# Seven block products in place of eight in the gate and up projections of a two-layer encoder trunk

## The chip, the core and the metric

The kernel runs on one core of a Trainium2 chip. The metric is the device time of one execution in microseconds. Before the change three runs took 2505.06 us in the median (2503.48 to 2505.37). About 0.2% (5 us) is what a measurement of this kernel can tell from no change.

## What is computed

Two groups of tokens, a prompt of 1024 and a sample of 32, go through a trunk of two layers of width 1024. The first layer mixes tokens with an mLSTM (a matrix-memory recurrence over chunks), the second with windowed attention. Each mixer is followed by a gated feed-forward block, and each of the four sub-layers ends in a layer norm. The part that the change touches is the feed-forward block:

```python
def swiglu(x, w_gu, w_down):
    g, u = jnp.split(x @ w_gu, 2, axis=-1)      # w_gu 1024 x 5632
    return (jax.nn.silu(g) * u) @ w_down        # w_down 2816 x 1024
...
x = layer_norm(DEEPNORM_ALPHA * x + swiglu(x, w_gu[layer], w_down[layer]), ln_g[layer, 1], ln_b[layer, 1])
```

Everything is float32.

## The kernel before, in words

**Layout.** Features lie on the partitions. The activations `act` are eight feature tiles of 128, each for three token groups of 384, 384 and 288 columns (`GRP`). A float32 product is made from exact halves: every operand is split into a high part in float32r and the remainder, and `gemm` (line 251) issues three matmuls for each 128-row step of the contraction: high by high (L256), low of the activations or weights by high (L257, L258). A product of a 128-wide weight tile with one group over 1024 features is therefore 24 matmuls.

**Weights.** The class `Weights` (line 110) streams units of 128 x 1024 in the order of their use through two raw buffers (`RAW`). A split is a copy on ScalarE (L143, tile `wh`) and a subtraction on GpSimd (L145, tile `wl`; a few on VectorE). A ring holds four split units. `done` frees a unit and splits the next while fewer than three live. Four of the eight units of an output projection get homes outside the ring.

**Feed-forward** (`ffn`, line 813). There are 22 tiles of 128 hidden features. For each tile and group, `up_group` makes the gate product and the up product (24 matmuls each), applies Silu on ScalarE (L827), multiplies on VectorE (L829) and splits the result into `hh` (L830, ScalarE) and `hl` (L831, VectorE). Tiles are taken in blocks of 2, 4, 4, 4, 4, 4. After the tiles of a block and the first tile of the next, `down` multiplies the block's hidden tiles with the down weights, for each of the eight output tiles and each group, and VectorE adds every result to `act` (L873 in the first block, L875 later). The products go through three PSUM banks (`psdense`). The last block's down products are in `norm_tail`, interleaved with the layer norm.

**Order of work.** The program is written out by hand, each engine takes its instructions in program order, and side work (norm, recurrence, attention) is a generator that `gemm` advances by a few instructions after each step of three matmuls (`Weave.tick`, which counts an estimate of the time). An instruction that waits holds up what is behind it on its engine.

Of the kernel before, what the change touches and what calls it, by code (L numbers as in the profile page):

```python
# [16 lines left out]
P = 128  # L17
# [14 lines left out]
BLOCKS = (2, 4, 4, 4, 4, 4)  # L32
# [6 lines left out]
RAW = 2  # L39
# [9 lines left out]
# token groups: moving columns of one matrix product  # L49
# [60 lines left out]
class Weights:  # L110
    """Streams weight units [128, w] and splits each into two float32r parts whose sum is exact."""

    def __init__(self, nc, pool, units):
        self.nc, self.pool, self.units = nc, pool, units
        self.nload = self.nsplit = 0
        self.raw, self.parts, self.home, self.live = {}, {}, {}, set()
        self.on_vector = set()

# [9 lines left out]

    def split_to(self, i):
        while self.nsplit <= i and self.nsplit < len(self.units):  # L130
            u = self.nsplit
            w = self.units[u].shape[-1]
            if u not in self.home and len(self.live) == 4:
                return
            self.load_to(u)
            r = self.raw.pop(u)
            if u in self.home:
                hi, lo = self.home[u]
            else:
                self.live.add(u)  # L140
                hi = self.pool.tile([P, WD], F32R, name=f"wh{u}", tag="wh", bufs=4)
                lo = self.pool.tile([P, WD], F32R, name=f"wl{u}", tag="wl", bufs=4)
            self.nc.scalar.copy(hi[:, :w], r[:, :w])  # L143
            eng = self.nc.vector if u in self.on_vector else self.nc.gpsimd
            eng.tensor_sub(lo[:, :w], r[:, :w], hi[:, :w].bitcast(F32))  # L145
            self.parts[u] = (hi, lo)
            self.nsplit += 1
            self.load_to(u + RAW)

    def get(self, u):  # L150
        self.split_to(u)
        return self.parts[u]

    def done(self, u):
        self.parts.pop(u)
        self.live.discard(u)
        while len(self.live) < 3 and self.nsplit < len(self.units) and self.nsplit - u < 12:
            self.split_to(self.nsplit)
# [3 lines left out]
def kernel(ctx: ExitStack, tc: tile.TileContext, A, O):  # L162
# [63 lines left out]
    W = Weights(nc, base, units)  # L226
    W.on_vector.update(U_Q[:1] + U_KV + U_QB[:1])

# [20 lines left out]
    scr_g, scr_x = per_tile(lambda g, n: dram.tile([P, KT, n], F32, name=f"scrx{g}"))  # L249

    def gemm(out, lhs, rhs):
        """out (+)= lhs.T @ rhs in float32 from exact halves: hi*hi + hi*lo + lo*hi."""
        last = len(lhs) - 1
        us = 3 * (max(out.shape[-1], 256) / 2400.0 + 0.003)
        for k, ((ah, al), (bh, bl)) in enumerate(zip(lhs, rhs)):
            nc.tensor.matmul(out, ah, bh, start=(k == 0), stop=False)  # L256
            nc.tensor.matmul(out, ah, bl, start=False, stop=False)  # L257
            nc.tensor.matmul(out, al, bh, start=False, stop=(k == last))  # L258
# [6 lines left out]
    def wcols(u, m=P):  # L265
        hi, lo = W.get(u)
        return [(hi[:, k * m : (k + 1) * m], lo[:, k * m : (k + 1) * m]) for k in range(KT)]
# [1005 lines left out]
```

## Time and profile before

| of the profiled execution | |
|---|---|
| span, first to last instruction (its own time) | 2505.9 us |
| median of the three timed runs | 2505.06 us |
| mean granted TensorE clock | 0.982 |
| TensorE busy | 2419.2 us, 14946 matmuls |
| VectorE / ScalarE / GpSimd busy | 939.1 / 786.6 / 696.2 us |
| HBM traffic over the span | 51 GB/s |

Matmuls overlap in the pipeline: a 128x384 matmul shows as some 340 ns but they start about 173 ns apart. The time that one costs is the distance between starts. Idle time of VectorE, ScalarE and GpSimd costs nothing by itself; what counts is whether TensorE waits.

### The profile page before, as it was taken

How to read it: one execution, taken by the hardware profiler on the slowest of the kernel's cores; microseconds unless marked ns; L12 is line 12 of the kernel's file. 1: busy time of each engine (PE TensorE's matmuls, PEld its weight loads, DVE VectorE, ACT ScalarE, POOL GpSimd, SP SyncE). 2: the span in 40 equal slices, each digit the busy share in tenths (PEclk: the TensorE clock that was granted, in tenths of full speed). 3: DMA queues.
4: the chain of work that ended last, by engine and by line, in shares of the span. 5: the costliest groups of instructions: out<-in, count | busy, mean ns of one | idle time of the engine just before them, and what ended most of it. 6: DMA issues, size and time to landing. Idle time of an engine off the chain costs nothing.

```text
span 2505.9 us, 36370 instructions
## 1 busy us (share of the span) xinstructions
PE 2419.2 (97%) x14946; PEld 2321.5 (93%) x14946; DVE 939.1 (37%) x2240; ACT 786.6 (31%) x1719; POOL 696.2 (28%) x545
## 2 busy tenths in 40 slices
PE   8999998999999999999979999898999999999997
PEld 8899898999999999999968888798999999999996
DVE  4444466542121212112275777655212121111227
ACT  3443444351211111121155677526121111212123
POOL 2443322341221312121253333225222121311222
PEclk9999999999999999999988999899999999999999
DMA  3221213011111111111121000210111110211111
GB/s 133 65 65 51 51 39 126 26 34 51 51 51 34 60 37 57 34 51 34 60 83 52 28 27 28 84 45 26 60 39 63 34 60 26 68 34 34 51 43 70
DMA packets 58901, 129.36 MB, mean 52 GB/s; under 512 B 8624, under 2 KB 32488, under 8 KB 58352
## 3 DMA queue, kind: packets, MB, share of 16 engines
q1 hardware_dynamic: 57008, 122.72, 15.0%
q10 hardware_dynamic: 1728, 4.33, 0.4%
q8 instruction: 117, 1.92, 0.3%
q14 instruction: 48, 0.39, 0.1%
HBM read 117.61 MB, written 9.41 MB: 51 GB/s over the span
## 4 chain that ended last, share of the span: by engine, by line
PE 85%; DVE 6%; ACT 3%; issue 2%; DMA 2%; POOL 2%; SPq 0%; POOLq 0%; DVEq 0%; ACTq 0%
PE d L256 26%; PE d L258 26%; PE d L257 25%; PE psS L1020 2%; PE T L1066 1%; PE psS L1019 1%; DMA wib<-scrw 1%; DVE sxl L280 1%; POOL wl L145 1%; DVE act L334 1%; PE O L1081 1%; PE O L1082 1%; DMA act<-in_x 1%; ACT junk L681 1%; PE ln L319 0%
## 5 line engine op out<-in xcount | busy, mean ns | idle before, releaser
L256 PE MATMUL d<-sxh,wh 128*128 128x384 f32 (+1 forms) x2928 | 971.2, 332 | 11.2 <-ACT sxh L279 7.1
L257 PE MATMUL d<-sxl,wh 128*128 128x384 f32 (+1 forms) x2928 | 950.0, 324 | 6.0 <-DVE sxl L280 6.0
L258 PE MATMUL d<-sxh,wl 128*128 128x384 f32 (+1 forms) x2928 | 952.4, 325 | 2.1 <-POOL wl L145 2.1
L145 POOL TENSOR_TENSOR wl<-wr,wh 128x1024 fp32r<-128x1024 f32 x170 | 408.7, 2417 | 1308.3 <-ACT wh L143 1286.5
L256 PEld LDWEIGHTS d<-sxh,wh 128*128 128x128 f32 x2928 | 555.9, 190 | 26.0 <-ACT sxh L279 7.7
L258 PEld LDWEIGHTS d<-sxh,wl 128*128 128x128 f32 x2928 | 556.1, 190 | 12.3 <-POOL wl L145 12.3
L257 PEld LDWEIGHTS d<-sxl,wh 128*128 128x128 f32 x2928 | 556.4, 190 | 9.0 <-DVE sxl L280 8.0
L829 DVE TENSOR_TENSOR t<-t,d 128x384 f32<-128x384 f32 x132 | 68.7, 521 | 781.9 <-PE d L258 780.0
L256 PE MATMUL d<-hh,wh 128*128 128x384 f32 (+1 forms) x1056 | 345.6, 327 | 10.6 <-DVE act L368 10.6
L257 PE MATMUL d<-hl,wh 128*128 128x384 f32 (+1 forms) x1056 | 342.6, 324 | 0.0
L258 PE MATMUL d<-hh,wl 128*128 128x384 f32 (+1 forms) x1056 | 342.2, 324 | 0.0
L143 ACT CAST wh<-wr 128x1024 fp32r<-128x1024 f32 (+1 forms) x174 | 177.3, 1046 | 257.6 <-PE d L257 195.6
L830 ACT CAST hh<-t 128x384 fp32r<-128x384 f32 x132 | 64.2, 486 | 506.3 <-DVE t L829 506.3
L256 PEld LDWEIGHTS d<-hh,wh 128*128 128x128 f32 x1056 | 199.3, 189 | 12.6 <-DVE act L368 11.5
L257 PEld LDWEIGHTS d<-hl,wh 128*128 128x128 f32 x1056 | 199.6, 189 | 1.1 <-issue 0.3
L258 PEld LDWEIGHTS d<-hh,wl 128*128 128x128 f32 x1056 | 199.4, 189 | 0.5 <-POOL wl L145 0.5
L875 DVE TENSOR_TENSOR act<-act,d 128x384 f32<-128x384 f32 (+1 forms) x192 | 100.1, 521 | 262.7 <-PE d L258 262.7
L827 ACT ACTIVATE t<-d 128x384 f32<-128x384 f32 x132 | 61.3, 465 | 398.6 <-PE d L258 398.5
L1042 POOL TENSOR_SCALAR s<-s,st 128x256 f32<-128x256 f32 (+2 forms) x72 | 65.6, 911 | 157.5 <-DVE st L1041 107.8
L831 DVE TENSOR_TENSOR hl<-t,hh 128x384 fp32r<-128x384 f32 x132 | 72.4, 548 | 77.2 <-ACT hh L830 77.2
L256 PE MATMUL d<-wh,sxh 128*128 128x256 f32 (+3 forms) x288 | 87.3, 303 | 0.0
L258 PE MATMUL d<-wh,sxl 128*128 128x256 f32 (+3 forms) x288 | 81.6, 283 | 0.0
(183 smaller groups left out, 2639.2 us busy)
## 6 DMA issues: line engine op xcount, KB each, us to landing
wr<-in_gu SPq DMA_DIRECT2D x88, 512.0 KB, 3.2
wr<-in_dn SPq DMA_DIRECT2D x44, 512.0 KB, 3.3
act<-in_x SPq DMA_DIRECT2D x3, 1536.0 KB, 8.0
wr<-in_wqk SPq DMA_DIRECT2D x8, 512.0 KB, 3.5
nm<-scrm SPq DMA_DIRECT2D x32, 128.0 KB, 4.0
wr<-in_wo SPq DMA_DIRECT2D x8, 512.0 KB, 4.3
wr<-in_wout_a SPq DMA_DIRECT2D x8, 512.0 KB, 3.2
wr<-in_wqb SPq DMA_DIRECT2D x8, 512.0 KB, 3.3
```

Source lines behind the costliest of these rows:

```text
L143: self.nc.scalar.copy(hi[:, :w], r[:, :w])
L145: eng.tensor_sub(lo[:, :w], r[:, :w], hi[:, :w].bitcast(F32))
L256: nc.tensor.matmul(out, ah, bh, start=(k == 0), stop=False)
L257: nc.tensor.matmul(out, ah, bl, start=False, stop=False)
L258: nc.tensor.matmul(out, al, bh, start=False, stop=(k == last))
L827: nc.scalar.activation(t, pg, AF.Silu)
L829: nc.vector.tensor_mul(t, t, pu)
L830: nc.scalar.copy(hh[i][:, t0 : t0 + n], t)
L831: nc.vector.tensor_sub(hl[i][:, t0 : t0 + n], t, hh[i][:, t0 : t0 + n].bitcast(F32))
L875: nc.vector.tensor_add(z[:], z[:], ps)
L1020: nc.tensor.matmul(psS[h][:R, lo:256], q[r, h, tk], KL[g2][r, kc], start=False, stop=True)
L1042: nc.gpsimd.tensor_scalar_mul(p[:R, 0, lo:256], p[:R, 0, lo:256], st[:R, 2, 0:1])
```

## The change

For 18 of the 22 tiles (2 to 19) the gate and up weights of a tile are one matrix of 2 x 2 blocks: gate tile over the first and the second 512 features (a1, a2), up tile likewise (b1, b2). The two groups of 384 tokens are the other matrix: X11, X21 (group 0, first and second 512 features), X12, X22 (group 1). Instead of eight block products the tile takes seven, each with one of seven weight factors: a1·X11, a2·X21, s2·T2, b2·T4, s1·T1, s3·T3 and s4·X22, where s1 = b1 + b2, s2 = s1 - a1, s3 = a1 - b1, s4 = a2 - s2, T1 = X12 - X11, T2 = X22 - T1, T3 = X22 - X12, T4 = X21 - T2. Group 2 (288 tokens) has its four block products as before, with a1, a2, b1, b2. Sums of products are made partly by accumulating in one PSUM bank (`A`), partly by copies on ScalarE and additions on VectorE.

- The T's are made once in each layer, at the start of the feed-forward block, by two generators (`comb`, `comb_4`). T1 is written over X12, whose split halves are first stored to DRAM and loaded back before tiles 20 and 21.
- The s's are made for every tile on VectorE, in place in the raw weight buffers (four operations of 128 x 512).
- A weight unit is now split in two halves of 128 x 512, each with its own ring slot. The ring has six half slots where there were four whole ones, and `done` refills while fewer than five halves live. There are three raw buffers.
- Blocks are nine of two tiles and one of four. Tiles 0, 1, 20 and 21 are done as before.
- Output projections have five homes instead of four, and `early` products in the second layer are three a group instead of four.

The functions `norm_tail`, `ln_task`, `mlstm` and `attention` are as before but for the ring. The diff, cut to its core (the rest removes comments, or renames):

```diff
-BLOCKS = (2, 4, 4, 4, 4, 4)
+BLOCKS = (2,) * 9 + (4,)
+SEVEN = range(2, FT - 2)
-RAW = 2
+RAW = 3
+SLOTS = 6
...
 class Weights:
+    FACTORS = ("a1", "a2", "b1", "b2", "s2", "s1", "s3", "s4")
...
+    def _source(self, u, f):
+        n = self.units[u].shape[-1] // 2
+        if f in (0, 1):
+            return self.raw[u][:, f * n : (f + 1) * n]
+        sub, add = self.nc.vector.tensor_sub, self.nc.vector.tensor_add
...
+        if f == "b2":
+            sub(a1, a1, b1)
+        elif f == "s2":
+            add(b1, b1, b2)
+            sub(b2, b2, a1)
+        elif f == "s1":
+            sub(a2, a2, b2)
+        return {"a1": a1, "a2": a2, "b1": b1, "b2": b2, "s1": b1, "s2": b2, "s3": a1, "s4": a2}[f]
...
+            hi = self.pool.tile([P, WD // 2], F32R, name=f"wh{u}_{f}", tag="wh", bufs=SLOTS)[:, :w]
+            lo = self.pool.tile([P, WD // 2], F32R, name=f"wl{u}_{f}", tag="wl", bufs=SLOTS)[:, :w]
+        self.nc.scalar.copy(hi, r)
+        eng = self.nc.vector if u in self.on_vector else self.nc.gpsimd
+        eng.tensor_sub(lo, r, hi.bitcast(F32))
...
+    def done(self, u, f=None):
+        for k in (0, 1) if f is None else (f,):
+            self.parts.pop((u, k))
+            self.live.discard((u, k))
+        while len(self.live) < SLOTS - 1 and self.njob < len(self.jobs) and self.jobs[self.njob][0] - u < 12:
+            if not self._next():
+                break
...
     def ffn(layer, li, tasks, lx, final):
...
+        def comb(lp):
+            for k in range(0, H, 2):
+                x11, x12 = (act_g[g][:, k : k + 2, :] for g in range(2))
+                x22 = act_g[1][:, k + H : k + H + 2, :]
+                t = new(lp, "acc", [P, 2, n0])
+                nc.vector.tensor_sub(t, x22, x12)
+                split_t(t, (th[1], tl[1]), k, nc.vector)
+                yield 1.2
+                t2 = new(lp, "sq", [P, 2, n0], bufs=2)
+                nc.vector.tensor_add(t2, t, x11)
+                split_t(t2, (th[0], tl[0]), k, nc.vector)
+                yield 2.4
+            for k in range(0, H, 2):
+                t = new(lp, "sq", [P, 2, n0], bufs=2)
+                nc.vector.tensor_sub(t, act_g[1][:, k : k + 2, :], act_g[0][:, k : k + 2, :])
+                split_t(t, t1, k, nc.vector)
+                yield 2.4
...
+        def up_seven(i, before=None):
...
+            a = new(psw, "A", [P, 512], bufs=2)[:, :n0]
+            mul(a, "a1", X11)
+            finish_tile()
+            gate0 = new(fp, "gate0", [P, n0])
+            nc.scalar.copy(gate0, a)
+            pg = psdense(2)
+            mul(pg, "a1", Y1, stop=False)
+            W.done(u, "a1")
+            b = new(psw, "B", [P, 512])[:, :n0]
+            mul(b, "a2", X21)
+            nc.vector.tensor_add(gate0, gate0, b)
+            nc.scalar.activation(gate0, gate0, AF.Silu)
+            mul(pg, "a2", Y2, start=False)
...
+            mul(pu, "b1", Y1, stop=False)
+            W.done(u, "b1")
+            mul(pu, "b2", Y2, start=False)
+            mul(a, "s2", T2, again=True)
+            W.done(u, "s2")
+            up0 = new(fp, "up0", [P, n0])
+            nc.scalar.copy(up0, a)
+            gated(i, 2, t2, pu)
+            def p4():
+                c = new(psw, "C", [P, 512])[:, :n0]
+                mul(c, "b2", T4)
+                W.done(u, "b2")
+                nc.vector.tensor_add(up0, up0, c)
+            if not before:
+                p4()
+            mul(a, "s1", T1, again=True)
+            W.done(u, "s1")
+            up1 = new(fp, "up1", [P, n0])
+            nc.scalar.copy(up1, a)
+            b = new(psw, "B", [P, 512])[:, :n0]
+            mul(b, "s3", T3)
+            W.done(u, "s3")
+            nc.vector.tensor_add(up0, up0, b)
+            nc.vector.tensor_add(up1, up1, b)
+            mul(a, "s4", X22, again=True)
+            W.done(u, "s4")
+            if before:
+                before()
+                p4()
+            def rest():
+                t = small(1)
+                nc.scalar.activation(t, a, AF.Silu)
+                gated(i, 0, gate0, up0)
+                yield 2.0
+                gated(i, 1, t, up1)
+            tail.append(wv.launch(rest()))
...
+            if g == 1:
+                for s, t in zip(scr_12, t1):
+                    nc.sync.dma_start(s[:], t.bitcast(F32))
+            if g == 2:
+                combs = wv.launch(comb(lx.scratch))
...
+        finish_tile()
+        fy.close()
+        for s, t in zip(scr_12, t1):
+            nc.scalar.dma_start(t.bitcast(F32), s[:])
```

The change moves instructions on the engines that feed TensorE. Three places matter below.

**First place: the start of the first feed-forward block.** On VectorE, from the products of group 1 on. `t`, `hl` are the gated result and its low half, `h0l`, `h1l` the same after the change, `acc` and `sq` scratch, `tl3`, `tl2` the low halves of T3 and T2. Before:

```order
L829 TENSOR_TENSOR t_720_5853<-t_720_5853,d_721_5855 128x384
L831 TENSOR_TENSOR hl_709_5686<-t_720_5853,hh_708_5685 128x384
L829 TENSOR_TENSOR t_723_5908<-t_723_5908,d_724_5910 128x288
L831 TENSOR_TENSOR hl_699_5602<-t_723_5908,hh_698_5601 128x288
L829 TENSOR_TENSOR t_726_5969<-t_726_5969,d_727_5971 128x288
L831 TENSOR_TENSOR hl_709_5686<-t_726_5969,hh_708_5685 128x288
L829 TENSOR_TENSOR t_731_6040<-t_731_6040,d_732_6042 128x384
L831 TENSOR_TENSOR hl_729_6014<-t_731_6040,hh_728_6013 128x384
```

After:

```order
L915 TENSOR_TENSOR t_728_5998<-t_728_5998,d_729_6000 128x384
L917 TENSOR_TENSOR h1l_720_5881<-t_728_5998,h1h_719_5880 128x384
L955 TENSOR_TENSOR acc_731_6032<-act1_76 128x768
L947 TENSOR_TENSOR tl3_704_5730<-acc_731_6032,th3_701_5727 128x768
L959 TENSOR_TENSOR sq_732_6045<-acc_731_6032,act0_75 128x768
L947 TENSOR_TENSOR tl2_703_5729<-sq_732_6045,th2_700_5726 128x768
L955 TENSOR_TENSOR acc_735_6070<-act1_76 128x768
L947 TENSOR_TENSOR tl3_704_5730<-acc_735_6070,th3_701_5727 128x768
L959 TENSOR_TENSOR sq_736_6086<-acc_735_6070,act0_75 128x768
L947 TENSOR_TENSOR tl2_703_5729<-sq_736_6086,th2_700_5726 128x768
L915 TENSOR_TENSOR t_733_6061<-t_733_6061,d_734_6063 128x288
L917 TENSOR_TENSOR h0l_715_5824<-t_733_6061,h0h_714_5823 128x288
```

Eight operations of 128 x 768 now stand ahead of the multiplication of tile 0, group 2 (`t_733`), and the split of a half of `T1` follows.

On ScalarE at the same place, around the weight copies for tile 2 (`wh36`). Before, up to the two copies after tile 1's last group:

```order
L827 ACTIVATE t_723_5908<-d_722_5883 128x288
L830 CAST hh_698_5601<-t_723_5908 128x288
L143 CAST wh36_5938<-wr36_5459 128x1024
L827 ACTIVATE t_726_5969<-d_725_5944 128x288
L830 CAST hh_708_5685<-t_726_5969 128x288
L143 CAST wh37_5999<-wr37_5599 128x1024
```

After (`th3`, `th2` are the high halves of T3 and T2):

```order
L946 CAST th3_701_5727<-acc_731_6032 128x768
L946 CAST th2_700_5726<-sq_732_6045 128x768
L926 ACTIVATE t_733_6061<-d_730_6028 128x288
L946 CAST th3_701_5727<-acc_735_6070 128x768
L946 CAST th2_700_5726<-sq_736_6086 128x768
L916 CAST h0h_714_5823<-t_733_6061 128x288
L184 CAST wh36_a1_6099<-wr36_5557 128x512
L184 CAST wh36_a2_6103<-wr36_5557 128x512
L184 CAST wh36_b1_6107<-wr37_5736 128x512
L946 CAST sxh1_79<-sq_738_6124 128x768
L926 ACTIVATE t_739_6140<-d_737_6111 128x288
L946 CAST sxh1_79<-sq_741_6152 128x768
```

The copy of the first factor a1 stands behind two splits of the T's and the cast `h0h` of tile 0's last group, which in turn waits for the VectorE row above.

**Second place: ScalarE at the end of the first feed-forward block**, where tile 19 ends and tile 20 begins. `wh90` to `wh93` belong to tiles 20 and 21, `t` is the gated result of a group. Before:

```order
L830 CAST hh_1035_10700<-t_1041_10782 128x384
L827 ACTIVATE t_1044_10837<-d_1043_10812 128x288
L830 CAST hh_1035_10700<-t_1044_10837 128x288
L143 CAST wh91_10867<-wr91_10608 128x1024
L143 CAST wh92_10873<-wr92_10698 128x1024
L827 ACTIVATE t_1049_10906<-d_1048_10881 128x384
L830 CAST hh_1046_10879<-t_1049_10906 128x384
```

After (`A` is the PSUM bank of tile 19, `scr12` the DRAM copy of X12):

```order
L184 CAST wh91_1_11762<-wr91_11672 128x512
L184 CAST wh92_0_11782<-wr92_11674 128x512
L1045 ACTIVATE t_1195_11786<-A_1183_11589 128x384
L916 CAST h1h_1190_11706<-gate0_1184_11602 128x384
L916 CAST h1h_1190_11706<-t_1195_11786 128x384
L1101 DMA sxh1_79<-scr120_87 128x1536
L1101 DMA sxl1_82<-scr121_88 128x1536
L926 ACTIVATE t_1199_11829<-d_1198_11804 128x384
L916 CAST h0h_1201_11856<-t_1199_11829 128x384
L926 ACTIVATE t_1204_11886<-d_1203_11861 128x384
```

The two loads that bring X12 back stand behind the last Silu and casts of tile 19, and ahead of the Silu of tile 20, group 0.

**Third place: GpSimd where the value projection of the second head pair ends**. `wl8` to `wl10` are the low halves of the next units, `qz`, `qwz`, `nm` belong to the recurrence. Before:

```order
L619 COPY qz0_202<-qT_38_731 64x128 x2
L625 TENSOR_TENSOR qwz0_205<-qT_38_731,wib_196_1633 64x128 x2
L626 TENSOR_TENSOR nm_195_1631<-nm_195_1631,cmask_119 128x256
L145 TENSOR_TENSOR wl9_1789<-wr9_882,wh9_1788 128x1024
L145 TENSOR_TENSOR wl10_1795<-wr10_966,wh10_1794 128x1024
```

After:

```order
L688 COPY qz0_214<-qT_38_757 64x128 x2
L694 TENSOR_TENSOR qwz0_217<-qT_38_757,wib_196_1667 64x128 x2
L695 TENSOR_TENSOR nm_195_1665<-nm_195_1665,cmask_121 128x256
L186 TENSOR_TENSOR wl8_1_1823<-wr8_751,wh8_1_1822 128x512
L186 TENSOR_TENSOR wl9_0_1829<-wr9_908,wh9_0_1828 128x512
L186 TENSOR_TENSOR wl9_1_1833<-wr9_908,wh9_1_1832 128x512
L186 TENSOR_TENSOR wl10_0_1839<-wr10_996,wh10_0_1838 128x512
```

Before, unit 8 (the next queries) had been split long ago at this point, and units 9 and 10 follow. After, the second half of unit 8 itself stands here.

More of the change, by code (lines that the diff above doesn't have):

```diff
@@ L127, in load_to @@
             self.nload += 1
-    def split_to(self, i):
[L130 to L148, printed above, removed]
+    def _source(self, u, f):
[3 more added lines that the diff above has]
+        sub, add = self.nc.vector.tensor_sub, self.nc.vector.tensor_add
+        a, b = self.raw[u], self.raw[u + 1]
+        a1, a2, b1, b2 = a[:, :n], a[:, n : 2 * n], b[:, :n], b[:, n : 2 * n]
+        if f == "b2":
[6 more added lines that the diff above has]
+        return {"a1": a1, "a2": a2, "b1": b1, "b2": b2, "s1": b1, "s2": b2, "s3": a1, "s4": a2}[f]
@@ L150, in get, with factor @@
+    def split_to(self, i):
+        while i < len(self.units) and self.njob <= self.last[i] and self._next():
+            pass
     def get(self, u):
         self.split_to(u)
[L152 to L158, printed above, removed]
+        return [self.parts[u, f] for f in range(2)]
+    def factor(self, u, f):
+        while (u, f) not in self.parts:
+            assert self._next()
+        return self.parts[u, f]
@@ L224 @@
     add_ffn(1)
-    W = Weights(nc, base, units)
+    W = Weights(nc, base, units, {up[i][0] for up in U_UP for i in SEVEN})
     W.on_vector.update(U_Q[:1] + U_KV + U_QB[:1])
@@ L249, with gemm @@
     scr_g, scr_x = per_tile(lambda g, n: dram.tile([P, KT, n], F32, name=f"scrx{g}"))
-    def gemm(out, lhs, rhs):
+    scr_12 = [dram.tile([P, KT // 2, GRP[1][1]], F32, name=f"scr12{i}") for i in range(2)]
+    def gemm(out, lhs, rhs, start=True, stop=True, again=False):
+        kw = {"skip_group_check": True} if again else {}
+        start, stop = start and not again, stop or again
         last = len(lhs) - 1
@@ L834, in up_group @@
                 W.done(uu)
+        tp = fy.enter_context(pool("comb"))
+        th = [new(tp, f"th{i}", [P, H, n0], F32R) for i in (2, 3, 4)]
+        tl = [new(tp, f"tl{i}", [P, H, n0], F32R) for i in (2, 3, 4)]
+        T2, T3, T4 = ([(h[:, k, :], l[:, k, :]) for k in range(H)] for h, l in zip(th, tl))
+        t1 = [t[1][:, :H, :] for t in (sxh_g, sxl_g)]
+        T1 = [(sxh[k][1][:], sxl[k][1][:]) for k in range(H)]
+        u4 = up[1][1]
+        W.home[u4] = tuple(t[2].rearrange("p k n -> p (k n)")[:, :D] for t in (th, tl))
@@ L877, in ffn @@
                     W.done(U_DN[layer][b][m // mpu])
+        finish_tile()
+        fy.close()
+        for s, t in zip(scr_12, t1):
+            nc.scalar.dma_start(t.bitcast(F32), s[:])
+        ep = fx.enter_context(pool("last"))
+        W.home[U_DN[layer][b][3]] = (new(ep, "dh", [P, D], F32R), new(ep, "dl", [P, D], F32R))
+        for i in tiles[2:]:
+            for g in range(3):
+                up_group(i, g)
         mpu = KT // kb
@@ L1144, in finish @@
         parts = wv.launch(to_parts(2, 1.2))
-    early = [(g, m) for g in range(2) for m in range(4)]
+    early = [(g, m) for g in range(2) for m in range(SLOTS // 2)]
     tasks, lx = mixer_out(U_OUT_B, 2, finish, early, before)
```

163 lines of the change are left out of this document (125 added, 38 removed).

## The prediction

> **What bounds the kernel now.** I read the page first (busy times and the chain that ended last), then the busy times by stretch, then the timeline of single stretches.
>
> ```profile
> span 2505.9 us, 36370 instructions
> PE 2419.2 (97%) x14946; PEld 2321.5 (93%) x14946; DVE 939.1 (37%) x2240; ACT 786.6 (31%) x1719; POOL 696.2 (28%) x545
> PE 85%; DVE 6%; ACT 3%; issue 2%; DMA 2%; POOL 2%; SPq 0%; POOLq 0%; DVEq 0%; ACTq 0%
> ...
> 560.00:1250.00 690.00, 689.99 (x4270) 684.93 (x4269) 134.60 (x253) 118.80 (x183) 145.55 (x61) 1.00 0.14 47
> 1757.00:2400.00 643.00, 642.99 (x3981) 638.51 (x3980) 120.66 (x232) 108.36 (x168) 133.57 (x56) 1.00 0.14 47
> ```
>
> The last two rows are the inner parts of the two feed-forward blocks. Their columns are TensorE, its weight loads, VectorE, ScalarE, GpSimd, then the granted clock. TensorE has no gap in 1333 us there, at full clock, and every other engine is under a quarter busy. Whatever takes matmuls out of these stretches shortens the span by their distance, as long as the others keep up. All waits of TensorE, some 80 us, lie elsewhere: in the mixers and where the norms meet the products.
>
> The distance of two matmuls comes from the starts in one stretch:
>
> ```profile
> 1099.96 0.34 PE L258 MATMUL d<-sxh,wl 128*128 128x384 f32 x1
> ...
> 1110.36 0.33 PE L258 MATMUL d<-sxh,wl 128*128 128x384 f32 x1
> 1110.53 0.29 PE L256 MATMUL d<-sxh,wh 128*128 128x288 f32 x1
> ...
> 1111.72 0.29 PE L256 MATMUL d<-sxh,wh 128*128 128x288 f32 x1
> ```
>
> The first two rows are 60 matmuls apart: 10.40 / 60 = 0.1733 us for 384 columns. The last two are 9 apart: 0.132 us for 288.
>
> **The seven products.** A tile had 2 units x 8 steps x 2 groups = 32 steps of three matmuls on the 384-token groups; it now has 7 x 4 = 28. Group 2 keeps its 16. So 12 matmuls go per tile, 18 tiles, two layers: 432 of the 13392 dense ones. At 0.1733 us that is **-74.9 us**. It all lies on the path, by the two rows above.
>
> **Blocks of two tiles.** The down products stay as many, but each result now sums two tiles instead of four, so VectorE's additions go from 144 to 240 a layer, and TensorE fills a bank in 1.04 us (six matmuls) instead of 2.08. The kernel already has one such block, its first:
>
> ```profile
> 583.00:606.00 23.00, 23.00 (x145) 23.00 (x144) 12.86 (x25) 4.44 (x5) 9.59 (x4) 1.00 0.28 92
> ...
> 589.77 0.56 DVE L873 SCALAR_TENSOR_TENSOR act<-act,d 128x384 f32<-128x384 f32 x1 [0.59 <-PE d L258]
> ...
> 592.68 0.56 DVE L873 SCALAR_TENSOR_TENSOR act<-act,d 128x384 f32<-128x384 f32 x1 [0.54 <-PE d L258]
> ```
>
> TensorE is gapless in it, and VectorE takes 12.86 of 23 us, waiting for TensorE before every addition. I take 0. What is new beside it is the tail of the tile before (two products, two low halves) and sums of weights; this I price in the last rival.
>
> **Sums, splits and copies in a steady tile.** The prices:
>
> ```profile
> L145 POOL TENSOR_TENSOR wl<-wr,wh 128x1024 fp32r<-128x1024 f32 x168 | 403.6, 2415 | 1298.5 <-ACT wh L143 1276.7 <-DVE aq L310 19.1 <-PE d L258 2.7
> L143 ACT CAST wh<-wr 128x1024 fp32r<-128x1024 f32 x172 | 175.2, 1046 | 257.6 <-PE d L257 195.6 <-DMA wr<-in_dn 46.4 <-DMA wr<-in_gu 12.3
> L875 DVE TENSOR_TENSOR act<-act,d 128x384 f32<-128x384 f32 x128 | 71.0, 555 | 196.4 <-PE d L258 196.4
> L831 DVE TENSOR_TENSOR hl<-t,hh 128x384 fp32r<-128x384 f32 x88 | 52.2, 593 | 55.3 <-ACT hh L830 55.3
> L830 ACT CAST hh<-t 128x384 fp32r<-128x384 f32 x88 | 45.2, 513 | 361.0 <-DVE t L829 361.0
> ...
> L827 ACT ACTIVATE t<-d 128x384 f32<-128x384 f32 x88 | 43.2, 491 | 309.8 <-PE d L258 309.7
> ...
> 508.79 0.96 DVE L334 TENSOR_TENSOR act<-act,rs 128x768 f32<-128x768 f32 x1
> ```
>
> Half a unit costs GpSimd 1.2 us and ScalarE 0.52. A tile with its down unit has ten halves: GpSimd 12 us, ScalarE 5.2 plus about 4.4 for copies, Silu and casts. VectorE has, per tile, four sums of 128 x 512 (0.64 each, two thirds of the last row), four additions of products (2.2), the gating (3.2) and 12 additions of down products (6.3): 14.3 us. TensorE needs 84 x 0.1733 + 48 x 0.132 + 11.5 = 32.4 us. No engine is over half busy. A factor is made up to five factors ahead of its use (some 8 us against 0.52 + 1.2), and the copies out of bank A stand beside a product of 2.08 us. I take 0; if one factor in each tile came 1 us late, that would be +36.
>
> **The start of the feed-forward block** is where I expect a wait. Free VectorE stands at 548.6 in the first layer:
>
> ```profile
> 548.02 0.56 DVE L831 TENSOR_TENSOR hl<-t,hh 128x384 fp32r<-128x384 f32 x1 [0.58 <-ACT hh L830]
> ...
> 511.13 0.83 ACT L344 CAST sxh<-act 128x768 fp32r<-128x768 f32 x1
> ...
> 553.27 0.45 DVE L829 TENSOR_TENSOR t<-t,d 128x288 f32<-128x288 f32 x1 [4.70 <-PE d L258]
> ...
> 553.76 0.43 ACT L830 CAST hh<-t 128x288 fp32r<-128x288 f32 x1 [3.35 <-DVE t L829]
> ...
> 559.40 0.34 PE L256 MATMUL d<-sxh,wh 128*128 128x384 f32 x1
> ```
>
> By the order, four half-steps of the T's come now, each VectorE 0.96, ScalarE 0.83, VectorE 0.96, one after the other: 11.0 us, to 559.6. Then the product of tile 0, group 2 (0.45) and its cast (0.43), and only behind it on ScalarE the copy of a1 (0.52), then GpSimd's half (1.2): 562.2. TensorE, which has the products of tile 1 to do until 559.40, wants that low half at its third matmul, 559.75. So it waits 2.5 us at least, say 3. Behind this, VectorE and ScalarE have T1 (two half-steps, 5.5), four sums (2.6) and T4, and the copy of `up0`, which s1·T1 waits for, stands behind them: another 0 to 3 us. A pause of this size also costs clock:
>
> ```profile
> 413.32 0.44 PE L256 MATMUL d<-sxh,wh 128*128 128x384 f32 x1 [1.73 <-ACT wh L143]
> ...
> 415.77 0.69 PE L258 MATMUL d<-sxh,wl 128*128 128x384 f32 x1 [1.83 <-POOL wl L145]
> ...
> 415.00:422.00 7.00, 6.23 (x20) 6.24 (x21) 7.00 (x8) 3.03 (x5) 5.06 (x3) 0.51 0.24 77
> ```
>
> After two pauses of under 2 us TensorE ran 7 us at 0.51 of its clock, which is 3.4 us lost. The slower pace hides part of the second wait. I take 6.5 us a layer, **+13**; 0 (if the half-steps come quicker) to 12 a layer.
>
> The Trainium skill (TensorE: Matmul & The Clock Gate, Part 1) has the clock fall to half after an idle window of about 3.4 us, and rise after a busy one. The trace agrees with the halving and with stretches of about 7 us, but shows it after pauses shorter than that. By the page's rule a wait of 3 us would mostly keep the clock, and this term would be 3 us a layer lower.
>
> **The end of the feed-forward block.** X12 comes back in two loads of 768 KB, which stand on ScalarE behind Silu (0.49) and two casts, the second behind VectorE's work: issued about 2.7 us after tile 19 ends.
>
> ```profile
> act<-in_x SPq DMA_DIRECT2D x3, 1536.0 KB, 8.0
> ...
> wr<-in_gu SPq DMA_DIRECT2D x88, 512.0 KB, 3.2
> ...
> 424.72 8.27 DMA wr<-in_wout_a
> ```
>
> 1536 KB landed in 8.0 us, so the low halves are there at 10.7. Tile 20, group 0 covers 48 x 0.1733 = 8.3. The wait is 2.4 us, with the clock 5.5: **+11** for both layers. If both land in 5.6 us it is 0; if they meet other loads as in the last row (a 512 KB unit beside the reload of x took 8.27 in place of 3.2), it is up to 14 a layer.
>
> **Half units elsewhere.** With five halves alive, only half of the next unit is ready where two units were in use together: twice for each head pair in the first mixer, and twice at the end of each feed-forward block. The second half is then wanted 12 x 0.1733 + 0.35 = 2.43 us after the first matmul. In the third place of the order:
>
> ```profile
> 145.59 0.34 PE L256 MATMUL d<-sxh,wh 128*128 128x384 f32 x1
> ...
> 147.79 1.98 ACT L143 CAST wh<-wr 128x1024 fp32r<-128x1024 f32 x2
> ```
>
> ScalarE gets to the split 2.2 us after TensorE begins; with 0.52 + 1.2 the half is there at 3.9, 1.5 late. Elsewhere ScalarE is nearer. Twelve such seams between 0 and 1.6 us: 0 to 19, I take 0.6 each, **+7**. The third raw buffer, the moved home and the shorter `early` list I take at 0: TensorE's waits there are for loads and norms that stay.
>
> **Sum.** -74.9 + 13 + 11 + 7 = -43.9. From the profiled execution's 2505.9 that is 2462.0; it stands 0.8 over the median of the runs, so against the median **2461 us**.
>
> **Rivals.**
>
> *Everything hides.* The T's and the reload come quicker, seams close: costs of 0 to 15, 2430 to 2445. For it: VectorE and ScalarE are mostly idle; against: the order puts a1 behind a serial chain.
>
> *Factors come late in every tile.* s2 needs two VectorE sums, a copy and a split in a row (3.0 us) and waits for b2's split. 1 us a tile gives 2497. For it: three engines must act in turn, each in order; against: the five factors of lead.
>
> *VectorE and GpSimd block each other in the down stages*, and the kernel ends slower. The rows:
>
> ```profile
> 512.77 1.44 DVE L391 TENSOR_TENSOR acc<-acc,act 128x288 f32<-128x288 f32 x1
> 514.13 3.47 DVE L334 TENSOR_TENSOR act<-act,rs 128x768 f32<-128x768 f32 x2
> ...
> 516.74 3.14 POOL L145 TENSOR_TENSOR wl<-wr,wh 128x1024 fp32r<-128x1024 f32 x1
> ```
>
> Beside GpSimd the 0.96 us operation takes 1.73, and GpSimd's 2.4 become 3.14. In a two-tile down stage of 23 us VectorE has 12.5 of additions, 2.2 of gating and 1.9 of sums; seven of these read two SBUF tensors. If each waited for a whole lengthened half split (1.57), VectorE would need 27.6, 4.6 too many: 18 stages, +83, 2544. It turns slower than before when a stage loses 2.7 us. Against it: GpSimd has only some four halves to split in a stage. The Trainium skill (SBUF — State Buffer, Terms) has the pair of ports of these two engines locked for a whole instruction, with the loser stopped. The rows above agree with it; by the page alone this rival would be the rule, and it speaks against this change.
>
> That the saving is not there at all needs matmuls that the order does not hold: it has 12960 dense ones.
>
> **Chances.** Forecast (2445 to 2480) 0.60, everything hides 0.16, late factors (2480 to 2500) 0.13, blocked engines 0.11, of which 0.03 ends within 0.2% (5 us, what a measurement can tell) and 0.08 slower. So faster 0.89, same 0.03, slower 0.08. The range 2435 to 2494 holds the forecast, most of the first rival and of the second; its ends are costs of 5 and of 64 us, where the bounds of the three terms together reach 71.
>
> **What would show it.** Right: 432 dense matmuls fewer, still 0.1733 us apart, no gap in the steady tiles; `d`/`A` of tile 2 waiting on `wh` or `wl` for about 3 us in each layer; a wait for the reloaded `sxl` at tile 20, group 1. Wrong: TensorE waiting on `act` additions (VectorE) in down stages, or on `wl` in tiles 3 to 19, or a clock below 0.97 in mean.

## The result, and the profile after

The changed kernel takes 2447.35 us in the median of four runs (2445.25 to 2448.07), the kernel before 2505.22 beside it: a ratio of 0.9768 with a 95% interval of 0.9754 to 0.9782, or 57.9 us less. The forecast was 2461, with a range of 2435 to 2494. Two slow executions are left out of every comparison: one of the kernel before (2939 us, at a mean granted clock of 0.75) and one of the kernel without the product s4*X22 (12355 us).

The head of the page of the changed kernel, and the busy times in the inner parts of its two feed-forward blocks (columns as in the prediction):

```profile
span 2445.7 us, 37323 instructions
PE 2346.8 (96%) x14514; PEld 2253.5 (92%) x14514; DVE 1245.9 (51%) x2772; ACT 941.4 (38%) x2173; POOL 926.5 (38%) x867
...
620.00:1150.00 530.00, 530.00 (x3312) 529.78 (x3311) 231.40 (x419) 155.47 (x309) 213.57 (x165) 1.00 0.15 50
1780.00:2340.00 560.00, 560.00 (x3490) 559.77 (x3489) 238.38 (x431) 163.55 (x326) 220.30 (x169) 1.00 0.16 52
```

There are 432 matmuls less (14946 to 14514), and in 1090 us of steady tiles TensorE again has no gap and full clock. VectorE and GpSimd are now busy for some 40% of these stretches, up from under a quarter. The distance of two matmuls of 384 columns is as before: 0.175 us in the mean of the starts between 620 and 1150 us, in both kernels. These two rows are 36 apart, 6.31 / 36 = 0.1753 us:

```profile
1102.57 0.34 PE L320 MATMUL C<-tl,wh_b 128*128 128x384 f32 x1
...
1108.88 0.33 PE L320 MATMUL A<-sxl,wh_s 128*128 128x384 f32 x1
```

The waits of TensorE that are new in the feed-forward blocks stand at the start of tile 2 in both layers, in the first down stage, at the reload of X12 in the first layer, and at the half-unit seams (the places where one weight unit follows another and only half of it is split). Rows of its timeline, with the idle time before each and its releaser:

```profile
559.41 0.44 PE L319 MATMUL A<-sxh,wh_a 128*128 128x384 f32 x1 [1.41 <-ACT wh_a L184]
561.38 0.45 PE L321 MATMUL A<-sxh,wl_a 128*128 128x384 f32 x1 [1.35 <-POOL wl_a L186]
572.90 0.45 PE L321 MATMUL A<-th,wl_s 128*128 128x384 f32 x1 [0.69 <-POOL wl_s L186]
577.10 0.69 PE L319 MATMUL A<-sxh,wh_s 128*128 128x384 f32 x1 [2.16 <-ACT up L1017]
...
590.59 0.44 PE L319 MATMUL d<-h0h,wh 128*128 128x384 f32 x1 [0.45 <-DVE act L1093]
...
1165.22 0.44 PE L320 MATMUL d<-sxl,wh 128*128 128x384 f32 x1 [1.49 <-DMA sxl<-scr]
...
1183.07 0.44 PE L321 MATMUL d<-sxh,wl 128*128 128x384 f32 x1 [0.54 <-POOL wl L186]
...
1724.85 0.44 PE L319 MATMUL A<-sxh,wh_a 128*128 128x384 f32 x1 [1.37 <-ACT wh_a L184]
1726.82 0.44 PE L321 MATMUL A<-sxh,wl_a 128*128 128x384 f32 x1 [1.35 <-POOL wl_a L186]
1742.49 0.44 PE L319 MATMUL A<-sxh,wh_s 128*128 128x384 f32 x1 [1.57 <-ACT up L1017]
1750.25 0.41 PE L319 MATMUL C<-th,wh_b 128*128 128x384 f32 x1 [0.82 <-DVE tl L947]
```

From start to start these waits are a little longer than the idle time shown (1.70, 1.69, 1.02, 2.50 us for the first four, less the usual distance of 0.17 each). Where the time went by stage is read from the first matmul that uses a stage's first weight unit, in each profiled execution; the last norm counts from the last matmul ahead of TensorE's first wait for it (us):

| stage | before | after | difference |
|---|---|---|---|
| up to the first feed-forward block | 512.1 | 510.4 | -1.7 |
| first feed-forward block | 780.3 | 756.4 | -23.9 |
| keys, attention, its output | 416.0 | 409.0 | -7.0 |
| second feed-forward block | 767.7 | 738.7 | -29.0 |
| last norm | 29.8 | 31.1 | +1.3 |
| span | 2505.9 | 2445.7 | -60.2 |

Each block saves 37.4 us of matmuls and gives 13.5 and 8.4 back.

### The profile page after: what moved, and what is told of

Its sections match the earlier page's. It is cut to its first block, busy times and chain, and to the rows that moved or that the text cites. A ratio compares the mean times of both kernels' runs of the same rounds, so it can differ in the third digit from the quotient of the medians.

```text
span 2445.7 us, 37323 instructions
## 1 busy us (share of the span) xinstructions
PE 2346.8 (96%) x14514; PEld 2253.5 (92%) x14514; DVE 1245.9 (51%) x2772; ACT 941.4 (38%) x2173; POOL 926.5 (38%) x867
## 5 line engine op out<-in xcount | busy, mean ns | idle before, releaser
L319 PE MATMUL d<-sxh,wh 128*128 128x384 f32 (+1 forms) x1104 | 382.4, 346 | 18.7 <-ACT wh L184 9.5
L186 POOL TENSOR_TENSOR wl<-wr,wh 128x512 fp32r<-128x512 f32 (+1 forms) x184 | 242.5, 1336 | 378.9 <-ACT wh L184 377.9
L320 PE MATMUL d<-sxl,wh 128*128 128x384 f32 (+1 forms) x1104 | 362.6, 328 | 3.9 <-DMA sxl<-scr 1.5
L321 PE MATMUL d<-sxh,wl 128*128 128x384 f32 (+1 forms) x1104 | 362.3, 328 | 3.9 <-POOL wl L186 3.0
L186 POOL TENSOR_TENSOR wl_s<-wr,wh_s 128x512 fp32r<-128x512 f32 x144 | 185.8, 1306 | 378.4 <-ACT wh_s L184 378.4
L319 PEld LDWEIGHTS d<-sxh,wh 128*128 128x128 f32 x1104 | 211.6, 192 | 33.4 <-ACT wh L184 10.6
L320 PEld LDWEIGHTS d<-sxl,wh 128*128 128x128 f32 x1104 | 212.2, 192 | 6.8 <-DVE sxl L348 2.5
L321 PEld LDWEIGHTS d<-sxh,wl 128*128 128x128 f32 x1104 | 211.6, 192 | 6.2 <-POOL wl L186 4.8
L319 PE MATMUL d<-h2h,wh 128*128 128x384 f32 (+1 forms) x384 | 124.5, 324 | 0.0
L321 PE MATMUL d<-h2h,wl 128*128 128x384 f32 (+1 forms) x384 | 124.1, 323 | 0.0
```

The source lines that it names most:

```text
L186: eng.tensor_sub(lo, r, hi.bitcast(F32))
L319: nc.tensor.matmul(out, ah, bh, start=start and k == 0, stop=False, **kw)
L320: nc.tensor.matmul(out, ah, bl, start=False, stop=False, **kw)
L321: nc.tensor.matmul(out, al, bh, start=False, stop=stop and k == last, **kw)
```

## The experiments

My theory was that the matmuls taken out are all on the path, and that what is given back lies at the ends of the blocks (chain of the combinations, reload, seams), not in the steady tiles. The rivals were port contention in the short down stages, factors that come late, and a hidden gain or loss from ring, raw buffers and blocks. Times in the expectations are compared with 2447 for the changed kernel; all ratios are to the kernel before on the same chip.

**Two-tile blocks alone**, in the kernel before:

```diff
-BLOCKS = (2, 4, 4, 4, 4, 4)
+BLOCKS = (2,) * 9 + (4,)
```

> The kernel before with one edit: its feed-forward blocks are the two-tile ones of the changed kernel, so VectorE makes 240 instead of 144 additions of down products a layer, and TensorE does the same matmuls. My theory: the smaller blocks cost nothing, since no addition in the changed kernel was waited for between tiles 3 and 19; 2505 us, within 3. The rival that VectorE and GpSimd block each other in the short down stages: 2.7 us or more in each of 18 stages, 2550 and over, with TensorE waiting for act.

2502.58 us, ratio 0.9987 (0.9978 to 0.9997). The stretch of the two layers that holds the short stages:

```profile
620.00:1200.00 580.00, 580.00 (x3607) 577.12 (x3607) 152.66 (x294) 97.64 (x152) 119.43 (x50) 1.00 0.14 46
1790.00:2380.00 590.00, 590.00 (x3666) 587.12 (x3665) 155.71 (x300) 98.15 (x153) 118.85 (x50) 1.00 0.13 44
```

TensorE has no gap. The blocks cost nothing; the feed-forward stages are 1.6 and 2.3 us shorter than before, if anything.

**Only the seven products undone**, ring, raw buffers and blocks kept (tiles 2 to 19 go through `up_group`, as in the kernel before, and the combinations, the copies and the reload of X12 are gone):

```diff
+        def up_eight(i):
+            for g in range(3):
+                up_group(i, g)
...
-                up_seven(tiles[1])
+                up_eight(tiles[1])
...
```

> The changed kernel with only the seven products undone: every tile takes the eight products again, no combinations T are made, X12 is neither put away nor reloaded; half-unit ring, third raw buffer, two-tile blocks and the shorter early list stay. My theory: 432 matmuls at 0.1733 us come back (+74.9), and the waits at the start of the feed-forward blocks (6.2 and 5.7 us of gaps, 1.7 and 1.5 of clock) and at the reload (1.7) go (-17): 2447 + 75 - 17 = 2505, and the attention stage keeps the 7 us by which it is shorter in the changed kernel (409 against 416 us), since ring, buffer and list make these. Rival: these 7 us come from the seven products' other phase, so that the attention stage is back at 416 and the time is 2512. If the products had been only partly on the path, the time would be under 2495.

2514.85 us, ratio 1.0037 (1.0023 to 1.0052): above both numbers, and neither account was right. The attention stage is 409.0 us, as my theory had it, so the rival fell. But the feed-forward blocks take 790.0 and 773.5 us, 9.7 and 5.8 more than before. The cause stands in its waits (total, count and longest of those between 620 and 1200 us) and in one seam (timeline of ScalarE, GpSimd and TensorE):

```profile
PE d L321 <- POOL wl L186: 4.8, 9, 0.5
...
698.63 2.17 ACT L184 CAST wh<-wr 128x512 fp32r<-128x512 f32 x4
...
699.32 3.77 POOL L186 TENSOR_TENSOR wl<-wr,wh 128x512 fp32r<-128x512 f32 x3 [28.62 <-ACT wh L184]
...
700.66 0.45 PE L321 MATMUL d<-sxh,wl 128*128 128x384 f32 x1 [0.53 <-POOL wl L186]
```

Wherever two whole units are in use together, the half-unit ring leaves the second half of the next unit to be split when TensorE is already in it. That is 0.70 us from start to start, 11 times in each layer: 15.4 us in all, against 15.5 measured in the two stages. So the half-unit ring with whole-unit products is a loss. With seven products it is not, since a factor is half a unit: of these eleven seams only the two at the end of a block are left. Against this kernel the seven products are worth 67.5 us.

**One product less**: s4*X22 is left out (its factor is still made):

```diff
-            mul(a, "s4", X22, again=True)
+            W.factor(u, "s4")
```

> The changed kernel with the product s4*X22 left out in the 18 tiles (its factor is still made; up1 for 384 tokens of the second group lacks that term): another 432 matmuls less. My theory: the steady tiles are set by TensorE alone, and would be with less of it: -74.9, so 2372 us, within 3, with no gap in tiles 3 to 19. Rival (late factors): the chain of sums, copies and splits for eight factors is just hidden at 32.4 us a tile; at 30.3 a tile it shows, and the saving is under 60 us: 2388 or more, with TensorE waiting for wl.

2398.1 us, in one execution: 49 us less and not 75. The saving is not whole, as the rival had it, but for another reason: no factor is late in the steady tiles. The waits between 611 and 1150 us, and VectorE's rows at the start of a down stage:

```profile
PE d L319 <- DVE act L1095: 5.8, 8, 0.7
...
650.14 0.99 DVE L915 TENSOR_TENSOR gate<-gate,up 128x384 f32<-128x384 f32 x1
651.71 0.56 DVE L917 TENSOR_TENSOR h1l<-gate,h1h 128x384 fp32r<-128x384 f32 x1 [0.58 <-ACT h1h L916]
652.19 1.01 DVE L1095 TENSOR_TENSOR act<-act,d 128x384 f32<-128x384 f32 x2
653.12 0.55 DVE L915 TENSOR_TENSOR t<-t,up 128x384 f32<-128x384 f32 x1
```

The gating of the tile before stands between the first additions of down products, on the same engine; three banks fill, and TensorE waits (0.84 and 0.24 us from start to start, in each of 16 stages: 17 us). In the changed kernel the 2.1 us of s4*X22 cover this. By these numbers its steady tile is gapless with some 1 us to spare at that place (2.1 less the two waits, an estimate), though VectorE is idle for more than half of the time. In tile 2, where b2*T4 comes last, the missing product also lets T4 come late:

```profile
584.20 0.41 PE L319 MATMUL C<-th,wh_b 128*128 128x384 f32 x1 [3.27 <-DVE tl L947]
```

With the other waits of tile 2 this makes 8.2 us a layer, where the changed kernel has 6.2 and 5.7: 4.5 more of the 26 that are missing. Two more stretches at half clock there (1.7 each), and a wait of 1.3 for the reload in the second layer, make up the rest.

**Each addition of down products made twice** (the second one into a scratch tile):

```diff
                         nc.vector.tensor_add(z[:], z[:], ps)
+                        nc.vector.tensor_add(new(fp, "x", [P, 384])[:, : GRP[g][1]], z[:], z[:])
```

> The changed kernel with each of VectorE's additions of down products in the middle blocks followed by a second SBUF addition of the same size into a scratch tile that nobody reads: 24 more of about 0.52 us in each two-tile down stage of 23 us, so VectorE goes from some 13 of 23 us there to some 26. By the theory that VectorE has room of about 9 us in a stage and no more, this overfills it by 3 us a stage or more, partly made up in the 65 us tile stretch: 2450 to 2500. If the port that VectorE and GpSimd share set the pace already, every stage would grow by the full 12.5 us: 17 stages, +200. If VectorE has room for all of it, 2447.

2505.06 us, ratio 0.9995 (0.9983 to 1.0006): 57.7 over the changed kernel, and above the 2450 to 2500 of my theory. The added operations, by form:

```profile
L1096 DVE TENSOR_TENSOR x<-act 128x384 f32<-128x384 f32 x256 | 166.4, 650 | 8.7
...
L1096 DVE TENSOR_TENSOR x<-act 128x288 f32<-128x288 f32 x128 | 70.5, 551 | 4.4
```

They are 236.9 us in 16 stages (the expectation counted 17), 14.8 in each; 57.7 / 16 = 3.6 come through, and the two feed-forward stages are 28.7 us longer each, which is the same. So some 11 of the 14.8 us found room on VectorE (9 by my theory), and port contention does not set the pace of the changed kernel: under that rival the whole addition would have shown.

**T2 and T3 one token group earlier**:

```diff
...
+                comb_23 = wv.launch(comb(lx.scratch))
             if g == 2:
-                combs = wv.launch(comb(lx.scratch))
+                wv.drain(comb_23)
+                combs = wv.launch(comb_1(lx.scratch))
```

> The changed kernel with the combinations T2 and T3 launched one token group earlier (beside the group-1 products of tiles 0 and 1, where VectorE and ScalarE stand idle for most of the time), so that only T1 stands ahead of the gating of tile 0, group 2, and of the copies of a1, a2 and b1. My theory: the serial chain of the combinations on VectorE and ScalarE is the whole cost of the start. Its waits (6.2 us in the first layer and 5.7 in the second, with 1.7 and 1.5 us of lost clock behind them) go: 2447 - 12 to -15, so 2432 to 2435 us, and TensorE waits neither for wh_a nor for wl_a. Rival: the chain then stands ahead of the norm of group 2, whose work on the same two engines comes later, and TensorE waits there instead: 2443 to 2452.

2453.2 us, ratio 0.9802 (0.9781 to 0.9823): the rival, and worse than it. The waits for `wh_a` and `wl_a` are gone as expected, but others stand in their place, at tile 0, group 2:

```profile
546.99 0.40 PE L319 MATMUL d<-sxh,wh 128*128 128x288 f32 x1 [0.30 <-ACT sxh L412]
548.47 0.61 PE L320 MATMUL d<-sxl,wh 128*128 128x288 f32 x1 [1.08 <-POOL sxl L413]
551.43 0.61 PE L319 MATMUL d<-sxh,wh 128*128 128x288 f32 x1 [1.39 <-ACT sxh L412]
552.91 0.61 PE L320 MATMUL d<-sxl,wh 128*128 128x288 f32 x1 [0.87 <-POOL sxl L413]
```

They are for the norm's output (L412, L413), which the combinations now push back. The clock also stood at half for 10.2 and 13.7 us there in the two layers (in these rows the last number but two is the granted clock):

```profile
548.00:559.00 11.00, 8.26 (x32) 7.60 (x33) 6.48 (x9) 5.27 (x9) 1.82 (x2) 0.53 0.00 0
1715.00:1730.00 15.00, 11.00 (x42) 9.50 (x42) 9.54 (x11) 6.02 (x11) 2.60 (x2) 0.54 0.00 0
```

VectorE is idle there for much of the time, but only while it waits for its partner; each step of a serial chain holds up what is queued behind it.

**The same combinations in pairs**, at their old place: both sums first, then both splits, beside the changed kernel once more:

```diff
-                split_t(t, (th[1], tl[1]), k, nc.vector)
-                yield 1.2
                 t2 = new(lp, "sq", [P, 2, n0], bufs=2)
                 nc.vector.tensor_add(t2, t, x11)
+                split_t(t, (th[1], tl[1]), k, nc.vector)
                 split_t(t2, (th[0], tl[0]), k, nc.vector)
...
```

> The changed kernel once more, beside the next two kernels on the same chip: 2447 us, within 3 (every theory).

> The changed kernel with the combinations made in another order, at the same place and in the same number: T3 and T2 of two feature tiles are summed first and then split, and so are the two sums of T1, so that VectorE no longer stands 0.90 us idle behind each cast of ScalarE. VectorE's chain ahead of the copy of a1 gets 11.0 - 7.7 = 3.3 us shorter, and the whole chain to the sums for s2 about 5 us. My theory: the serial chain at the start sets the waits there; then the two waits for a1 (3.0 us of gaps a layer) go wholly and the later ones (3.2 and 2.7) shrink to 0 to 1.5, with the clock stretch behind them: 5 to 7 us a layer, so 2433 to 2437 us, without the group-2 waits that the earlier launch made. Rival: the chain of the factors (GpSimd's halves, VectorE's sums for s2) is behind it, and what a1 gains comes back as a longer wait for s2: 2443 or more.

The changed kernel again took 2447.23 us, 0.9766 (0.9753 to 0.978); the paired one 2440.45, 0.9736 (0.9722 to 0.9749), between the 2433 to 2437 of my theory and the rival's 2443. VectorE's rows of the changed kernel, then those of the paired one:

```profile
547.02 0.95 DVE L955 TENSOR_TENSOR acc<-act 128x768 f32<-128x768 f32 x1
548.87 0.96 DVE L947 TENSOR_TENSOR tl<-acc,th 128x768 fp32r<-128x768 f32 x1 [0.90 <-ACT th L946]
...
557.93 0.45 DVE L915 TENSOR_TENSOR t<-t,d 128x288 f32<-128x288 f32 x1
```

```profile
548.34 0.95 DVE L955 TENSOR_TENSOR acc<-act 128x768 f32<-128x768 f32 x1
549.39 0.96 DVE L957 TENSOR_TENSOR sq<-acc,act 128x768 f32<-128x768 f32 x1
...
555.85 0.45 DVE L915 TENSOR_TENSOR t<-t,d 128x288 f32<-128x288 f32 x1
...
560.02 4.00 DVE L947 TENSOR_TENSOR sxl<-sq,sxh 128x768 fp32r<-128x768 f32 x2
```

The gating (L915) comes 7.5 us after the first sum and not 10.9, and the waits for a1 are gone in both layers. The later ones are not; TensorE's rows of the paired kernel:

```profile
570.84 0.44 PE L321 MATMUL A<-th,wl_s 128*128 128x384 f32 x1 [0.62 <-POOL wl_s L186]
575.03 0.69 PE L319 MATMUL A<-sxh,wh_s 128*128 128x384 f32 x1 [2.16 <-ACT up L1017]
...
1732.84 0.45 PE L321 MATMUL A<-th,wl_s 128*128 128x384 f32 x1 [0.61 <-POOL wl_s L186]
1737.02 0.44 PE L319 MATMUL A<-sxh,wh_s 128*128 128x384 f32 x1 [2.17 <-ACT up L1017]
```

So both had a part. The first two waits, 3.0 us a layer, were the chain ahead of a1; with them gone the kernel is 6.8 us faster. (The two feed-forward stages are 4.4 and 3.3 us shorter; 1.2 of the 4.4 is a shorter wait at the reload, which differs between executions of the same kernel too.) The later waits stay in the first layer and grow by 1.4 in the second, since TensorE now comes to them about as much earlier as the chain does. In this kernel T1's two splits take 4.00 us, where two of 0.96 would do, beside GpSimd's halves. The further gain of the chain was lost there.

**The reload earlier**, behind the copy of `up1` of tile 19, alone and with the pairs:

```diff
+        def reload():
+            for s, t in zip(scr_12, t1):
+                nc.scalar.dma_start(t.bitcast(F32), s[:])
...
             nc.scalar.copy(up1, a)
+            if i == FT - 3:
+                reload()
...
-        for s, t in zip(scr_12, t1):
-            nc.scalar.dma_start(t.bitcast(F32), s[:])
```

> The changed kernel with the two loads that bring X12 back issued from ScalarE right behind the copy of up1 of tile 19, which is as early as their place is free (s1*T1 is its last reader), and not behind the whole tile. My theory: the reload costs the 1.7 us of one wait for sxl in the first layer and nothing in the second, so 2447 - 1.7 = 2445 us, which only the profile can tell, by that wait being gone. Rival, by the term of the forecast: the reload holds 11 us in pauses and clock that the list of gaps does not show as its own; 2436 us.

> The kernel with the paired order of the combinations and the early reload of X12 together. My theory: the two gains add up, since they lie at different ends of the feed-forward block: 1 to 2 us under the paired kernel, 2431 to 2436 us, and no wait for sxl at the end of the first block. Rival: as in the paired kernel alone, 2441 or more.

2446.63 us, ratio 0.9766 (0.975 to 0.9783), and with the pairs 2440.15, 0.9737 (0.9724 to 0.975). ScalarE's rows in the first of these kernels, which issues the loads 6.2 us earlier after the start of the block (640.6 us behind it in place of 646.7):

```profile
1149.80 0.48 ACT L1035 COPY up<-A 128x384 f32<-128x384 f32 x1 [1.66 <-PE A L321]
1149.81 0.34 ACTq L985 DMA_DIRECT2D sxh<-scr  x1
```

No wait for `sxl` is left, in either kernel, and the time moves by less than can be told, so the rival's 11 us were not there. The reload cost the one wait that the profile shows, 1.7 us in this execution of the changed kernel and 1.1 in the other one that was profiled. The last kernel has the lowest time of all, cannot be told from the paired one, and misses the 2431 to 2436 expected of it.

**Raw buffers and ring**: two raw buffers alone in one kernel, and in another also seven places in the ring (this diff):

```diff
-RAW = 3
+RAW = 2
-SLOTS = 6
+SLOTS = 7
```

> The changed kernel with two raw weight buffers in place of three, and nothing else changed. My theory: nothing, 2447 us, within 3, since no wait of TensorE in the changed kernel is for a raw unit; in the seven-product tiles both units of a pair must stay until the eighth factor is made, and the next unit (512 KB, some 3.6 us) still comes in time within 32 us. Rival: with both raw buffers held by one pair, the down unit and the next pair come late in every tile, 1 to 4 us in each of 36: 2483 to 2590.

> The changed kernel with seven half-unit places in the ring in place of six, and two raw buffers in place of three, so that both fit in SBUF. With six halves alive a second unit is whole when the first one is used. My theory: the seams go (two at the end of each feed-forward block and the ones in the first mixer, 0.7 us each where the profile shows them, some 4 us in all), and the third raw buffer is worth nothing: 2443 us. Rival: the raw buffer is what shortens the attention stage, by up to 7 us: 2450.

2458.17 us, ratio 0.9814 (0.98 to 0.9829), and 2458.41, 0.9819 (0.9802 to 0.9836). My theory that the third buffer is worth nothing fell: it is 11 us, and the kernel with seven places lies above both numbers expected of it. The rival's waits in every tile are not there either; the steady tiles have no gaps. With six places 8.2 us of it lie ahead of the first feed-forward block and 3.4 in the attention stage, which is within what that stage varies. Some 5 of the 8.2 can be found in the trace. With two buffers ScalarE's weight copy waits three times for the load of value weights (`in_wv`), 13.1 us in all; in the changed kernel it never does. TensorE's next wait for the recurrence behind each of them is 1.3 to 1.9 us longer than in the changed kernel. At the second the chain can be read: a copy of the recurrence (`act`, L773) stands behind the weight copy on ScalarE, VectorE's `act` waits for that, and TensorE for VectorE. For the other two, and for the rest, the cause is not shown:

```profile
154.85 0.62 ACT L184 CAST wh<-wr 128x512 fp32r<-128x512 f32 x1 [4.51 <-DMA wr<-in_wv]
...
156.01 0.44 PE L726 MATMUL T<-vt,ks 128*64 128x129 f32 x4 [1.31 <-DVE act L774]
```

With seven places none lies ahead of that block (508.2 us), 6.8 lie in the attention stage, 2.8 in the first feed-forward block and 4.5 in the second, where s2*T2 waits 2.24 us for the copy of `gate0` and s1*T1 3.89 for the copy of `up0`. The seven places did close the seams at the ends of the blocks, as forecast.

## Why the prediction was right, point by point

- **Seven products, -74.9.** Right: 432 matmuls, at 0.175 us where 0.1733 was used, all on the path. The kernel with eight products again shows it from the other side: 67.5 us more, where 75 back, 13 for its eighteen additional seams and 18 less for the start, the first down stages and the reload would make 70.
- **Two-tile blocks, 0.** Right; alone they gain some 3.6 us, hardly more than can be told. One sign that the prediction had put down as "wrong" did show, TensorE waiting for `act` in a down stage, but only in the first one of each layer (0.45 and 0.47 us).
- **Steady tiles, 0.** Right, but the reason (no engine over half busy) was too weak: the kernel with six products shows that the margin is 1 us, at the first additions of a down stage, while the averages are all low.
- **Start of the block, +13.** Measured 6.2 and 5.7 us of gaps and some 1.7 and 1.5 of lost clock: +15. The wait for a1, forecast at 3, is 3.05 and 3.0. The second was at the upper end of its "0 to 3" (3.2 and 2.7). The clock cost less than the 3.4 us of the example that it was taken from, but not nothing. In the first layer it stood at half for 3.4 us, not 7, from this second wait on:

```profile
577.00:581.00 4.00, 3.90 (x14) 3.90 (x15) 2.92 (x5) 1.29 (x4) 1.76 (x2) 0.58 0.40 133
```

- **Reload, +11.** The wait was right, the size wrong: 1.7 us, in one layer. The loads were issued at 1157.17, 2.0 us behind the last Silu of tile 19 (forecast: 2.7 behind the tile), and the wait was 1.49 instead of 2.4:

```profile
1155.18 0.49 ACT L1045 ACTIVATE t<-A 128x384 f32<-128x384 f32 x1 [1.59 <-PE A L321]
1157.17 0.34 ACTq L1101 DMA_DIRECT2D sxh<-scr  x1
1157.55 1.32 ACTq L1101 DMA_DIRECT2D sxl<-scr  x1
```

  The 3.1 us of clock that were added to it a layer did not come: this pause left the clock alone. In the second layer there was no wait. By the times of their packets both loads were done 7.7 us after the first was issued in the first layer, and 5.7 in the second; 5.6 was the prediction's own bound for no wait at all. Why the two differ stays open.
- **Seams, +7.** Four stand at the ends of the blocks, at 0.70 each (2.8 us). In the first mixer two of the eight show, of 0.73 and 0.74 us of idle time, the first of them at the named third place (151.08 us), where 1.5 was worked out. That mixer as a whole is no longer than before.
- **Raw buffer, home, shorter list, 0.** Wrong by itself: the third raw buffer is worth 11 us in this kernel, and the attention stage is 7.0 us shorter, which the eight-product kernel has as well (409.0). Up to 4 of these 7 are uncertain, since kernels with the same code in that stage took 409.0 to 413.0 there. What repeats in every run stands right behind the attention: with the old ring, home and list TensorE waits there for `sxl` three times (0.94, 1.85 and 1.84 us), in every other kernel once (0.3), with two raw buffers as with three. So the third buffer is not what makes this part; home, list and ring were not tested apart.
- **Why 14 under the forecast.** The reload (9 less), the attention stage (7 less), the seams (4 less) and the stretch ahead of the first block (2 less) outweigh the start (2 more) and what was not forecast at the norms and the first down stages (4 more). The larger errors point the same way, so the time did not fall into the range by errors that cancel.
- **The rivals.** That everything hides (2430 to 2445) did not come true, but the time is nearer to it than to the forecast's middle. Late factors did not appear between tiles 3 and 19. Contention between VectorE and GpSimd is there, and does not reach TensorE in the steady tiles:

```profile
L917 DVE TENSOR_TENSOR h2l<-gate,h2h 128x384 fp32r<-128x384 f32 x16 | 14.6, 911 | 16.0 <-ACT h2h L916 16.0
...
L917 DVE TENSOR_TENSOR h1l<-t,h1h 128x384 fp32r<-128x384 f32 x18 | 10.1, 559 | 10.4 <-ACT h1h L916 10.4
```

  The same operation takes 911 ns in the mean in one place and 559 in another. Of the 88 of this line and shape in the changed kernel, the 20 that overlap an instruction of GpSimd take 765 to 1341 ns, the other 68 all 557 to 561. The Trainium skill (SBUF — State Buffer, Terms) has the loser of the shared ports stopped for the whole of the other's instruction. These rows agree with it, and so do the 4.00 us of T1's splits in the paired kernel; that it would decide the time here does not follow, as the doubled additions show.

The measured parts of the spans add up: -75 for the matmuls, +15 start, +1.2 first down stages, +1.7 reload, +2.8 seams at the ends of the blocks, +1.9 for a longer wait at the norm at the end of the first block, -7.0 attention stage, -1.7 ahead of the first block, +1.3 last norm: -60, against -60.2.

## What to carry to other kernels

Where TensorE has no gap, taking matmuls out pays by their distance until the margin of the others is used up (the second 432 paid 49 us and not 75). What is given back is to be looked for at the seams, where a pipeline is filled or drained: price the queue of each engine there instruction by instruction, and not its mean load. Here a chain between two engines was better shortened by issuing two of its links side by side (7 us gained) than moved to an earlier place (6 us lost), because what was moved pushed something else back. A staging size that costs 15 us with one consumer (half units with whole-unit products) can be free with another, so each part of a change is worth measuring with and without the rest.

## What the runs showed of the hardware

- The half-clock stretches of TensorE have lengths of 3.4, 6.8, 10.2, 13.7 and 20.5 us in the records of these runs: multiples of 3.4, but for the one at the end that the record cuts off. Two pauses of 1.4 and 1.35 us in a row were followed by one in the second layer of the changed kernel and by none in the first, and the single pause of 1.49 at the reload by none. The pause of 2.2 us for `up0` in the first layer came with one in the paired kernel and with none when the early reload was added to it. The Trainium skill (TensorE: Matmul & The Clock Gate, Part 1) has a window of about 3.4 us that runs freely, and half clock after an idle one. The lengths agree with the window; the pauses here were all shorter than it, and the same pause with two outcomes would fit a window that runs freely.
- A 128 x 512 half split on GpSimd was forecast at half of the whole unit's 2.4 us. It took 1.31 us in the mean where little stood beside it, and in places more where VectorE worked; the second row, from the start of tile 2, is two splits of 1.93 beside the sums for T1:

```profile
L186 POOL TENSOR_TENSOR wl_s<-wr,wh_s 128x512 fp32r<-128x512 f32 x144 | 185.8, 1306 | 378.4 <-ACT wh_s L184 378.4
```

```profile
559.44 3.86 POOL L186 TENSOR_TENSOR wl_a<-wr,wh_a 128x512 fp32r<-128x512 f32 x2 [15.84 <-ACT wh_a L184]
```
